# First squares on ScalarE, key-cache split spread over steps, samples' set-up later in each head: a hybrid decoder step on one core

## The chip, the cores and the metric

The kernel runs on one core of a Trainium2 chip. The metric is the device time of one execution, in microseconds (us); each comparison uses the median of several executions. Engines are named as the profile names them: PE is TensorE's matmul, PEld its weight load, DVE is VectorE, ACT is ScalarE, POOL is GpSimd, SP is SyncE, whose queue issues every DMA here.

## The reference

One layer of a decoder with three parallel branches is computed for a prompt of 1024 tokens and for 8 samples of 4 tokens, with the same weights, in float32. Cut to what matters:

```python
h = rmsnorm(x) * g;  p = h @ w_in      # ret q,k,v,g | sgu u,v | xattn q | 3 gates
A = silu(g) * groupnorm(retention(rope(q), rope(k), v))       # 4 heads, chunks of 128
B = gelu(u) * (tril(W_s) @ layernorm(gelu(v)) + b)            # per chunk of 128 positions
C = softmax(xq @ mem_k.T / sqrt(128)) @ mem_v                 # 4 heads, 256 memory rows
x = x + (sig(gA)*A@w_br_ret + sig(gB)*B@w_br_sg + sig(gC)*C@w_br_x) @ w_o
x = x + convffn(rmsnorm(x));   y = rmsnorm_final(x)
```

The mean square of x that the first norm needs is a sum over 1024 features, which lie on 8 tiles of 128 partitions. For the samples, retention starts from a given state of each head, and cross-attention reads a given cache of keys and values; both need masked copies of the samples' queries, one copy for each of the 8 samples.

## The kernel before

All 1056 tokens (1024 of the prompt, 32 of the samples) lie along the free dimension; features lie on partitions. Every float32 operand of a matmul is split into a rounded high part and a remainder, and a product takes three matmuls: high by high, high by low, low by high. The high part is a copy on ACT, the remainder a subtraction, for weights mostly on POOL (`w_prep`, lines 140 to 155: tiles `wh` and `wl`, three of each). The input is kept unnormalised in the split (`hh`, `hl` from the raw tiles `xr`, function `x_part`, lines 392 to 396); the reciprocal root `rst` of the mean square is multiplied in afterwards, when a product is taken out of the accumulation memory.

A product of 8 feature tiles is made by `fm`: eight steps of nine matmuls (three terms by three column chunks). After each step `hook()` is called. It runs deferred single operations (`later(n, ...)`, due after n hooks) and then, at the current `rate`, advances a queue of Python generators, `gens`, by one `yield` each. What lies between two yields of a generator is thus put between two steps of matmuls in PE's order and at that point of every other engine's order. [...] `drain()` runs the generators to their end.

The first two products, q and k of head 0, are interleaved by `fm2` over 16 steps, so that PE can follow the arrival of x. q's tile is complete at the 13th step and is then taken out by `rope_evac` (ACT copies `sw`, DVE multiplies by `cosT`, POOL multiplies `sw` by `sinT`, and DVE adds the two four hooks later). The tile pool for products, `mp`, has two buffers, so the third product, g of head 0, starts only once q's buffer has been read. The smaller pool `ap` has two buffers of one bank each.

In the ramp the sum of squares is made in two parts. Tiles 0 to 3 are squared and added on POOL, ahead of everything in `gens` (lines 408 to 411). Tiles 4 to 7 are squared on ACT and added on DVE inside the generator `xnorm` (lines 428 to 465), after `YA` empty yields; after `YB` further ones it forms `rst` by `rstd_all` (split the sum into `rsh` and `rsl`, three pairs of matmuls with a matrix of ones, three Newton operations on DVE), transposes it into `rtok`, takes g's tile out of the accumulation memory, and multiplies `q`, `k`, `cosT` and `sinT` by `rst`. During head 0 the rate is one yield per hook, and 32 hooks lie in q, k and the two g products. If g has not been taken out by then, lines 714 and 715 step `xnorm` until it has; then `drain()` runs the rest.

Each head's `retention` generator runs during the next head's products, at 25.5/32 of a yield per hook. Its operations are A (scores of two chunks; four DVE operations and one on ACT make the tile `rt`), B (one chunk's output and state), C (transposing two chunks back), and for the samples SA (set-up: masked scores, `kdm` on POOL, and in heads 0 to 2 the masked queries `qm3`, two DVE multiplications by a mask), SC (samples' products with the state; it reads `qm3`), SB and SD. B and SA are two of the operations that use the two `ap` buffers in turn. At each operation's start, deferred normalisations of earlier rows (DVE, after a POOL power) are issued first.

Before the cross-attention, `KS(0, 0)` and `KS(0, 1)` split the first key cache (ACT copies `kch`, POOL subtractions `kcl`) where they stand, after the product `sv`. `gens` then holds `sgu`, whose steps multiply on PE, add on DVE (`sgt`) and multiply on DVE (`su`), and `xattn(0)`, whose product YA is the first to read the keys. Three `xq` products and eight `gb` products, 88 hooks at 1.05 yields each, cover `sgu` and the four `xattn` generators.

Of the kernel before, what the change touches and what calls it, by code (L numbers as in the profile page):

```python
# [10 lines left out]
AF = mybir.ActivationFunctionType  # L11
ALU = mybir.AluOpType
# [66 lines left out]
def step_kernel(ctx: ExitStack, tc: tile.TileContext, xT, memT, wslab, cst, ident_d, rope, vec, sgc, sgm, sgs,  # L79
# [10 lines left out]
    def slot(name, dt=F32, shape=None):  # L90
        return sp.tile(shape or [P, T], dt, tag="S", name=name, bufs=NSLOT)
# [16 lines left out]
    def act(out, in_, func=AF.Identity, scale=1.0, bias=0.0, **kw):  # L108
        nc.scalar.activation(out=out, in_=in_, func=func, scale=scale, bias=bias, **kw)  # L109

    def vtt(out, a, b, op):
        nc.vector.tensor_tensor(out=out, in0=a, in1=b, op=op)  # L112

    def ptt(out, a, b, op):
        nc.gpsimd.tensor_tensor(out=out, in0=a, in1=b, op=op)  # L115
# [56 lines left out]
    gens = deque()  # L172
# [112 lines left out]
    def split(src, name, sub=ptt):  # L285
        shape = list(src.shape)
        hi = slot(name + "h", F32R, shape)
        lo = slot(name + "l", F32R, shape)
        nc.scalar.copy(out=hi, in_=src)
        sub(lo, src, f(hi), ALU.subtract)  # L290
        return hi, lo
# [60 lines left out]
    with tc.manual_schedule():  # L352
# [9 lines left out]
        xr = [slot("xr") for _ in range(8)]  # L362
# [43 lines left out]
            x_part(k, slice(0, T))  # L406

        for k in range(4):
            ptt(xr[k], xr[k], xr[k], ALU.mult)
            for a, b in {1: ((1, 0),), 3: ((3, 2), (3, 1))}.get(k, ()):  # L410
                ptt(xr[a], xr[a], xr[b], ALU.add)
        for i in range(2):
            hil[SLABS[i]] = first[i]
        wst.update(d=2, p=2, live=2)
# [8 lines left out]
        nc.vector.tensor_scalar(out=vecs[:, VBG:VBG + 32], in0=vecs[:, VBG:VBG + 32], scalar1=0.5, scalar2=None,  # L423
                                op0=ALU.mult)

        YA, YB = 5, 6

        def xnorm():
            for _ in range(YA):
# [64 lines left out]
        def retention(h, qt, kt, silu, V, st, s3, s0, s0s):  # L494
# [156 lines left out]
                    stt(ot[e][:, TP:T], a[:, e * 32:e * 32 + 32],  # L651
                        vecs[:, VGN + 2 * h + e:VGN + 2 * h + e + 1], silu[e][:, TP:T], ALU.mult, ALU.mult)

            for fn, *a in ((int,), (A, 0), (SA,), (A, 1), (B, 0), (B, 1), (SC, 0), (B, 2), (C, 0), (SC, 1), (A, 2), (B, 3),
                           (SB, 0), (B, 4), (C, 1), (A, 3), (B, 5), (SD,), (B, 6), (C, 2), (SB, 1), (B, 7),
                           (SB, 2), (SB, 3), (C, 3)):
                while defer:
                    defer.pop(0)()
                fn(*a)
                yield  # L660
# [37 lines left out]
        for h in range(H):  # L698
# [58 lines left out]
            tm((("v", h, 0), ("v", h, 1)), hops, v_evac, st[0:NSAMP, 256:512])  # L757
            drain()
            gens.append(retention(h, qt, kt, silu, V, st, s3, s0, s0s))


# [116 lines left out]
        def sgu():  # L878
            for _ in range(3):
                yield  # L880
            for half in range(2):
                for g in range(4):
                    a = ap()
                    for n in range(4):
                        mm(a[:, n * P:(n + 1) * P], vt(4 * half + n)[:, g * P:(g + 1) * P], sgW[:, g * P:(g + 1) * P])
                    t = slot("sgt")
                    vtt(t[:, 0:512].rearrange("p (a b) -> p a b", a=4), a.rearrange("p (a b) -> p a b", a=4),
                        sgC[:, g * P:(g + 1) * P].unsqueeze(1).to_broadcast([P, 4, P]), ALU.add)
                    s = su[g][:, half * 512:(half + 1) * 512]
                    vtt(s, s, t[:, 0:512], ALU.mult)  # L890
                    yield
                if half == 0:
                    vc_load(0)
            a = ap()
            for g in range(4):
                mm(a[:, g * 32:g * 32 + 32], sgS[0:32, 512 + g * P:512 + (g + 1) * P],
                   sgS[0:32, 256 + 32 * g:256 + 32 * g + 32])
            t = slot("sgt")
            vtt(t[:, 0:128], a[:, 0:128], sgC[:, 512:640], ALU.add)
            for g in range(4):  # L900
                ptt(su[g][:, TP:T], su[g][:, TP:T], t[:, g * 32:g * 32 + 32], ALU.mult)
                later(4, lambda g=g: dma(scr[8 + g], su[g]))
            yield
# [25 lines left out]
        def KS(h, i):  # L929
            if h < H:  # L930
                ksl.setdefault(h, {})[i] = split(kcl[h][i], "kc")
# [184 lines left out]
        later(4, lambda: dma(sgv, sgS[0:32, 512:1024]))  # L1116
        rate[0] = 1.05
        gens.append(sgu())
        KS(0, 0)
        KS(0, 1)  # L1120
        gens.append(xattn(0))
        for m in range(1, 4):
            xq_unit(m)
# [104 lines left out]
        def x_split(name, k, src, sub):  # L1228

            while len(X.setdefault(name, [])) <= k // 2:  # L1230
                X[name].append((slot("xh", F32R), slot("xl", F32R)))
            hi, lo = xop(name, k)
            nc.scalar.copy(out=hi, in_=src)
            if sub:
                sub(lo, src, f(hi), ALU.subtract)
# [27 lines left out]
        def h_scale(k, half):  # L1263
            stt(hs(k, half), hs(k, half), vecs[:, VNF + k:VNF + k + 1], rst[:, half * HW:(half + 1) * HW], ALU.mult, ALU.mult)
# [215 lines left out]
        A = lambda k: (h_scale(k, 1), x_split(B1(k), k % 4, h(k, 1), None))  # L1480
# [471 lines left out]
def build(shapes):  # L1952
    import concourse.bacc as _bacc

    nc = _bacc.Bacc("TRN2", target_bir_lowering=False, num_devices=1)
    args = [nc.dram_tensor(f"in_{n}", shapes[n], F32, kind="ExternalInput").ap() for n in _INS]
    args += [nc.dram_tensor(f"out_{n}", s, F32, kind="ExternalOutput").ap() for n, s in _OUTS]
    with tile.TileContext(nc) as tc:
        step_kernel(tc, *args)
    return nc  # L1960
# [22 lines left out]
```

## Time and profile before

| | us |
|---|---|
| median of 3 runs (1942.96 to 1952.96) | 1944.57 |
| the profiled execution's own time | 1949.1 |
| its span, first to last instruction | 1947.3 |
| PE busy | 1878.4 (96%) |
| DVE busy | 1078.1 (55%) |
| POOL busy | 927.7 (48%) |
| ACT busy | 615.9 (32%) |

A row of the timeline has the start and the length in microseconds, the engine, the line of the kernel, the operation, the tiles written and read, the shape and a count where equal instructions were merged (the length is then that of the whole series). In brackets stands how long the engine had been idle before it and whose work ended that. A row of a list of waits has the total, the number and the longest. A row by windows has the busy time of each engine in a stretch, then the granted TensorE clock as a share of full speed (PEclk).

### The profile page before, as it was taken

To read this page: it belongs to the slowest core of one execution; us is meant where nothing else is said; L and a number is where in the kernel's file an instruction comes from. 1 tells how busy PE (TensorE), PEld (TensorE's weight loads), DVE (VectorE), ACT (ScalarE), POOL (GpSimd) and SP (SyncE) were. 2 spreads that over 40 slices of the span, in tenths; PEclk is the share of its full clock that TensorE was granted. 3 is DMA by queue.
4 is the path that set the end of the run, shared out by engine and by line. 5 is a ranking of instruction groups with operands and counts; after the bars stand their busy time and mean duration, and the time that the engine had idled before them with its cause. 6 is when DMAs were issued, how large, how long until landed. Compare 5 with 4: busy or idle time off the path is not lost.

```text
span 1947.3 us, 31390 instructions
## 1 busy us (share of the span) xinstructions
PE 1878.4 (96%) x13201; PEld 1852.8 (95%) x13201; DVE 1078.1 (55%) x1506; ACT 615.9 (32%) x962; POOL 927.7 (48%) x576
## 2 busy tenths in 40 slices
PE   7999999999989999999999999899999999999997
PEld 6999999999989999999999999899999999999996
DVE  8463636443375541111112247999999999744446
ACT  5232232322234332111132233534434334321204
POOL 6242424232544334333154434477777777753404
PEclk9999999999999999999999999899999999999998
DMA  5112121324142313111221443022222222742202
GB/s 184 55 44 91 44 91 44 132 68 153 55 133 77 109 45 133 55 44 54 89 84 48 164 153 99 33 66 89 77 66 89 77 84 95 264 142 89 75 1 90
DMA packets 51741, 174.51 MB, mean 90 GB/s; under 512 B 5712, under 2 KB 8944, under 8 KB 51600
## 3 DMA queue, kind: packets, MB, share of 16 engines
q1 hardware_dynamic: 51600, 172.50, 26.3%
q8 instruction: 104, 1.70, 0.4%
q14 instruction: 37, 0.30, 0.1%
HBM read 137.04 MB, written 35.43 MB: 89 GB/s over the span
## 4 chain that ended last, share of the span: by engine, by line
PE 80%; DVE 11%; ACT 3%; issue 3%; DMA 1%; POOL 1%; SPq 0%; DVEq 0%; ACTq 0%; POOLq 0%
PE mp L106 55%; PE bp L106 20%; PE ap L106 4%; DVE xl L112 1%; DVE c L118 1%; DVE x2c L118 1%; DVE hl L118 1%; DVE s L112 1%; DMA xr<-in_xT 1%; DMA scr<-ox 0%; ACT sw L476 0%; DVE rt L118 0%; DVE st L526 0%; SPq L103 0%; PE ap L576 0%
## 5 line engine op out<-in xcount | busy, mean ns | idle before, releaser
L115 POOL TENSOR_TENSOR wl<-wr,wh 128x1024 fp32r<-128x1024 f32 x114 | 296.7, 2605 | 463.6 <-ACT wh L150 391.2
L106 PE MATMUL mp<-hh,wh 128*128 128x384 f32 (+1 forms) x1152 | 264.2, 337 | 9.7 <-DVE q L112 4.9
L106 PE MATMUL mp<-hl,wh 128*128 128x384 f32 (+1 forms) x1152 | 254.1, 328 | 4.8 <-DVE hl L118 4.8
L106 PE MATMUL mp<-hh,wl 128*128 128x384 f32 (+1 forms) x1152 | 251.8, 326 | 0.0
L106 PE MATMUL bp<-xh,wh 128*128 128x264 f32 (+2 forms) x1040 | 211.4, 284 | 1.0 <-DVE x2c L118 0.9
L106 PE MATMUL bp<-xl,wh 128*128 128x264 f32 (+2 forms) x1040 | 211.1, 284 | 0.0
L106 PE MATMUL bp<-xh,wl 128*128 128x264 f32 (+2 forms) x1040 | 211.0, 284 | 0.0
L106 PEld LDWEIGHTS mp<-hh,wh 128*128 128x128 f32 x1152 | 192.9, 192 | 12.9 <-ACT hh L109 5.3
L106 PEld LDWEIGHTS mp<-hl,wh 128*128 128x128 f32 x1152 | 193.5, 190 | 7.2 <-DVE hl L118 7.2
L106 PEld LDWEIGHTS mp<-hh,wl 128*128 128x128 f32 x1152 | 193.8, 190 | 0.0
L112 DVE TENSOR_TENSOR x<-x,mp 128x288 f32<-128x288 f32 (+3 forms) x167 | 105.7, 675 | 121.3 <-PE mp L106 121.3
L106 PEld LDWEIGHTS bp<-xh,wh 128*128 128x128 f32 x1040 | 162.4, 188 | 1.4 <-issue 1.4
L106 PEld LDWEIGHTS bp<-xl,wh 128*128 128x128 f32 x1040 | 162.4, 188 | 0.0
L106 PEld LDWEIGHTS bp<-xh,wl 128*128 128x128 f32 x1040 | 162.3, 188 | 0.0
L115 POOL TENSOR_TENSOR wl<-fs,wh 128x1024 fp32r<-128x1024 f32 x41 | 119.0, 2902 | 55.7 <-ACT wh L1295 55.7
L150 ACT CAST wh<-wr 128x1024 fp32r<-128x1024 f32 x100 | 103.9, 1041 | 78.7 <-PE mp L106 50.0
L106 PE MATMUL mp<-ach,whs 128*128 128x384 f32 (+3 forms) x524 | 124.3, 326 | 3.9 <-DVE x L112 3.1
L118 DVE SCALAR_TENSOR_TENSOR c<-z,hist,c 128x1024 f32<-128x1024 f32 x88 | 124.6, 1416 | 4.2 <-ACT c L109 2.5
L112 DVE TENSOR_TENSOR th<-mp,rst 128x768 f32<-128x768 f32 (+1 forms) x48 | 31.6, 701 | 170.9 <-PE mp L106 150.3
L106 PE MATMUL mp<-acl,whs 128*128 128x384 f32 (+3 forms) x524 | 124.1, 327 | 0.0
L106 PE MATMUL mp<-ach,wls 128*128 128x384 f32 (+3 forms) x524 | 124.0, 326 | 0.0
L118 DVE SCALAR_TENSOR_TENSOR th<-th,mp 128x768 f32<-128x768 f32 (+1 forms) x48 | 31.7, 701 | 145.4 <-PE mp L106 145.4
(356 smaller groups left out, 4107.9 us busy)
## 6 DMA issues: line engine op xcount, KB each, us to landing
wr<-in_wslab SPq DMA_DIRECT2D x162, 512.0 KB, 3.6
sca<-c SPq DMA_DIRECT2D x22, 528.0 KB, 3.0
opr<-sca SPq DMA_DIRECT2D x22, 528.0 KB, 4.5
opr<-scr SPq DMA_DIRECT2D x16, 528.0 KB, 5.4
scr<-ort SPq DMA_DIRECT2D x8, 528.0 KB, 7.6
x2c<-in_xT SPq DMA_DIRECT2D x8, 528.0 KB, 7.7
scx<-x2c SPq DMA_DIRECT2D x16, 264.0 KB, 3.5
x<-scx SPq DMA_DIRECT2D x8, 528.0 KB, 6.9
```

Of the source, the lines that this page charges most:

```text
L106: nc.tensor.matmul(out=out, lhsT=l, rhs=r, start=start, stop=stop)
L112: nc.vector.tensor_tensor(out=out, in0=a, in1=b, op=op)
L115: nc.gpsimd.tensor_tensor(out=out, in0=a, in1=b, op=op)
L118: nc.vector.scalar_tensor_tensor(out=out, in0=a, scalar=s, in1=b, op0=op0, op1=op1)
L150: nc.scalar.copy(out=hi, in_=raw)
```

## The change

Three places change. In the ramp, tiles 0 to 3 are squared on ACT instead of POOL and added on DVE instead of POOL; `xnorm` starts its own squares after 14 yields instead of 5, which is the second yield after q's tile is complete, and waits 3 yields instead of 6 before `rstd_all`. In each head the samples' set-up SA comes after both score operations and the first B instead of between the two A. In the cross-attention the split of the first key cache becomes a generator with two yields after each half, placed between `sgu` and `xattn(0)`.

```diff
         for k in range(4):
-            ptt(xr[k], xr[k], xr[k], ALU.mult)
+            act(xr[k], xr[k], AF.Square)
             for a, b in {1: ((1, 0),), 3: ((3, 2), (3, 1))}.get(k, ()):
-                ptt(xr[a], xr[a], xr[b], ALU.add)
+                vtt(xr[a], xr[a], xr[b], ALU.add)
...
-        YA, YB = 5, 6
+        YA, YB = 14, 3
...
-            for fn, *a in ((int,), (A, 0), (SA,), (A, 1), (B, 0), (B, 1), (SC, 0), (B, 2), (C, 0), (SC, 1), (A, 2), (B, 3),
+            for fn, *a in ((int,), (A, 0), (A, 1), (B, 0), (SA,), (B, 1), (SC, 0), (B, 2), (C, 0), (SC, 1), (A, 2), (B, 3),
...
         gens.append(sgu())
-        KS(0, 0)
-        KS(0, 1)
+
+        def first_keys():
+            for i in range(2):
+                KS(0, i)
+                yield
+                yield
+
+        gens.append(first_keys())
         gens.append(xattn(0))
```

## The prediction

> **What bounds the kernel.** I read the page's chain first, then the list of what PE waited for, then the timeline around each wait that the change touches, engine by engine.
>
> ```profile
> PE 80%; DVE 11%; ACT 3%; issue 3%; DMA 1%; POOL 1%; SPq 0%; DVEq 0%; ACTq 0%; POOLq 0%
> ...
> PE ap L106 <- DVE sgt L112: 7.6, 1, 7.6
> ...
> PE ap L106 <- DVE rt L118: 5.4, 3, 2.6
> PE mp L106 <- DVE q L112: 4.9, 1, 4.9
> ...
> PE mp L106 <- DVE hl L118: 4.8, 7, 1.7
> ```
>
> PE sets the time, so an edit is worth what it takes from PE's waits. The four rows are the waits that the change aims at: the masked products of `sgu`, the heads' `rt`, q's eviction and the splits of x. All four are waits for DVE.
>
> **The ramp, what goes away.** The rows are the timeline's, then one stretch by windows.
>
> ```profile
> 10.78 1.32 DVE L118 SCALAR_TENSOR_TENSOR hl<-xr,vecs,hh 128x1056 fp32r<-128x1056 f32 x1 [0.46 <-ACT hh L109]
> 12.18 18.90 POOL L115 TENSOR_TENSOR xr<-xr 128x1056 f32<-128x1056 f32 x6 [2.81 <-DVE hl L118]
> 13.23 18.96 DVE L118 SCALAR_TENSOR_TENSOR hl<-xr,vecs,hh 128x1056 fp32r<-128x1056 f32 x6
> 18.61 1.18 ACT L109 ACTIVATE hh<-xr,vecs 128x1056 fp32r<-128x1056 f32 x1
> ...
> 13.24 0.65 PE L106 MATMUL mp<-hh,wh 128*128 128x384 f32 x3
> 14.70 0.64 PE L106 MATMUL mp<-hh,wh 128*128 128x384 f32 x3
> 37.23 0.65 PE L106 MATMUL mp<-hh,wl 128*128 128x384 f32 x3
> 42.76 1.22 PE L106 MATMUL mp<-hh,wh 128*128 128x384 f32 x3 [4.89 <-DVE q L112]
> ...
> 42.00:48.00 6.00, 5.24 (x18) 5.27 (x19) 5.99 (x6) 5.00 (x7) 4.83 (x3) 0.50 0.28 87
> ```
>
> One split `hl` takes 1.32 with POOL idle. The six that run beside POOL's six squares and additions take 18.96, 3.16 each, and POOL's 3.15 each: the two engines take turns. Without POOL's six, the splits follow ACT's `hh`, whose last ends at 18.61 + 1.18 = 19.8, so the last split ends near 21.2 instead of 32.2. PE's steps are 14.70 - 13.24 = 1.46 apart. Twelve remain from 14.70, so q and k would end at 32.2; they end half a microsecond after 37.23, at 37.7. The earlier splits bring **5.5**. The new `hl` times (14.6, 15.9, 17.3, 18.6, 19.9, 21.2) are all ahead of the steps that read them, the next of which start at 15.2, 17.6 and 19.1.
>
> PE then waits until 42.76 for q's eviction, which stands behind DVE's additions: **5.0**. After the wait the clock is granted at 0.50 (42.00 to 48.00), with PE busy for 5.24: half of that, **2.6**, is lost too. Together 13.1.
>
> **The ramp, what comes.** The moved work is four squares and seven additions in all, and its order decides.
>
> ```profile
> 22.43 1.09 ACT L109 ACTIVATE xr<-xr 128x1056 f32<-128x1056 f32 x1 [2.64 <-DVE hl L118]
> 33.22 1.04 ACT L150 CAST wh<-wr 128x1024 fp32r<-128x1024 f32 x1
> 34.29 2.19 ACT L476 COPY sw<-mp 64x768 f32<-64x768 f32 x4
> ...
> 34.34 2.55 POOL L115 TENSOR_TENSOR wl<-wr,wh 128x1024 fp32r<-128x1024 f32 x1 [3.26 <-ACT wh L150]
> 36.85 3.42 POOL L115 TENSOR_TENSOR sw<-sw,sinT 128x1056 f32<-128x1056 f32 x1
> ...
> 41.31 1.31 DVE L112 TENSOR_TENSOR q<-mp,cosT 128x768 f32<-128x768 f32 x2
> ...
> 156.11 0.95 PE L106 MATMUL ap<-V,rt 128*128 128x256 f32 x6 [1.99 <-DVE ort L118]
> ...
> 157.40:160.90 3.50, 3.50 (x14) 3.50 (x13) 1.83 (x5) 0.37 (x1) 0.74 (x2) 0.51 0.51 206
> ```
>
> The first four squares, 1.09 each, run on ACT from 19.8 to 24.2, and the three additions at some 1.25 on DVE until about 29, the last held up by POOL's next weight split. q's tile is complete at 27.8; ACT's four copies (2.19) end at 30.1, DVE's eviction (1.31) at 30.5, both before 32.2. So g starts without a wait, with 1.7 to spare; if that cover went, each microsecond later would be one lost.
>
> From there I place the instructions in the new order, with 2.45 for a POOL operation and 1.25 for a DVE one, taking turns. ACT: a cast until 31.1, two squares until 33.3, k's copies until 35.5, a cast until 36.6, two squares until 38.7. POOL: weight split until 35.0, k's `sw` until 38.7, weight split until 42.3. DVE, each behind POOL's current one: first addition 36.2, k's eviction 37.6, q's sum 39.9, addition 43.6, two more 46.1, k's sum 47.3, `rsl` 48.5. In PE's order the matmuls of ones come after the ninth step from 32.2, at 45.3. They **wait 3.2**. This wait is new, since `xnorm` has been moved back by 6 yields. Its bounds: 0 if DVE need not wait for POOL (five additions of 1.25 and `rsl` end before 45), 7 if all seven operations take a turn of 3.3.
>
> The other end of `xnorm` moves as well: it needs 34 yields to g's eviction, and there are 32 hooks. The last transposes and that eviction come after all matmuls of the second g, and the next product needs g's buffer: copies of `rtok`, then 1.3 for the eviction as for q, **1.8** (bounds 1.3 and 3).
>
> [...] The ramp: 13.1 - 3.2 - 1.8 - 1.3 = **6.8**, between 2 and 11.5.
>
> [...]
>
> **The heads.** In heads 0 to 2, A, B and SA each move into the next one's place in PE's order.
>
> ```profile
> 101.51 4.93 POOL L115 TENSOR_TENSOR wl<-wr,wh 128x1024 fp32r<-128x1024 f32 x2 [13.88 <-ACT wh L150]
> 106.69 1.90 POOL L115 TENSOR_TENSOR kdm<-s,cB 96x1024 fp32r<-96x1024 f32 x1 [0.26 <-DVE s L112]
> ...
> 104.11 0.18 DVE L112 TENSOR_TENSOR st<-ap,cB 96x32 f32<-96x32 f32 x1
> 105.07 1.54 DVE L112 TENSOR_TENSOR s<-st,s 32x160 fp32r<-32x160 f32 x1 [0.79 <-ACT s L592]
> 106.75 2.46 DVE L112 TENSOR_TENSOR s<-s,cB 128x256 fp32r<-128x256 f32 x2
> 109.13 0.47 DVE L118 SCALAR_TENSOR_TENSOR rt<-ap,cB 128x256 fp32r<-128x256 f32 x1
> 110.43 0.42 DVE L112 TENSOR_TENSOR rt<-rt,cB 128x256 fp32r<-128x256 f32 x1
> 110.76 0.42 DVE L568 COPY Sst<-ap 128x256 f32<-128x256 f32 x1
> 113.21 0.42 DVE L526 TENSOR_SCALAR cB<-cB,mv,grs 128x256 f32<-128x256 f32 x1 [0.94 <-POOL grs L115]
> ...
> 106.98 0.87 PE L106 MATMUL ap<-V,rt 128*128 128x256 f32 x6
> 113.33 0.28 PE L106 MATMUL ap<-s0h,s 128*64 128x256 f32 x1
> ```
>
> SA holds DVE from 104.11 to 109.2, and the second A's `rt` follows it; the second B waits for its buffer. Moving SA removes these waits: 5.4 in three heads, and clock of about 1.1 expected for the one of 2.6. What is late next is SC, which reads the masked queries. In head 0 the second `rt` ends at 106.8 (its last operation behind POOL's splits, 101.51 + 4.93 = 106.4). B's row work with its normalisation, which is issued ahead of SA and waits for POOL's power, takes 113.63 - 110.76 = 2.9: 109.7. SA's chain took 5.1, of which 1.2 was the operation at 105.07 behind the weight split: 3.9, to 113.6, with `kdm` before the masked queries as now. SC stands at 113.33 less the removed wait of 1.4, 111.9: it waits 1.7. By the same steps head 2 waits about 2.2, head 1 about 0.5 (first B, `rt` not ready) and 1.6: 6.0 in all, with clock 2.4. The edit is worth 5.4 + 1.1 - 6.0 - 2.4 = **-1.9**, bounds +6.5 (no wait at SC) and -6 (1.4 more per head). Head 3 makes no split queries and no PE wait of it is listed: nothing.
>
> **The first keys.**
>
> ```profile
> 537.54 1.28 POOL L115 TENSOR_TENSOR sgS<-sgS,sgW 32x512 f32<-32x512 f32 x1 [0.71 <-DVE sgS L874]
> 538.79 4.66 POOL L115 TENSOR_TENSOR kcl<-kc,kch 128x1024 fp32r<-128x1024 f32 x2
> 543.42 4.62 POOL L115 TENSOR_TENSOR wl<-wr,wh 128x1024 fp32r<-128x1024 f32 x2
> ...
> 538.03 10.57 DVE L112 TENSOR_TENSOR su<-su,sgt 128x512 f32<-128x512 f32 x1
> ...
> 549.25 2.08 PE L106 MATMUL ap<-sgW,vg 128*128 128x128 f32 x8 [7.58 <-DVE sgt L112]
> ...
> 549.20:553.40 4.20, 4.15 (x16) 4.15 (x17) 3.37 (x5) 0.23 (x1) 0.00 (x0) 0.50 0.80 242
> ```
>
> A DVE multiplication that needs 0.7 stands for 10.57, from inside POOL's `sgS` until POOL's whole series ends at 548.0: here there is no taking of turns. PE waits 7.58 and then runs at 0.50 for 4.2, losing 2.1: 9.7. Without `kcl` the two weight splits follow `sgS` at 538.8 and end at 543.4, so the multiplication ends at 544.0 and the next eviction at 544.7; PE, done at 541.7, waits 3.1 plus clock 1.3. Gain 9.7 - 4.4 = **5.3**; bounds 9.7 (turns) and 0. The two `kcl`, 4.66, come behind `sgu`'s last step, two yields apart, when DVE has only q's split and mask for `xattn`; I take 0 there, since the first comes four steps ahead of these, and up to 2.5 if a POOL operation holds them up. The tail fits: `xattn` moves back four yields, 92 of 92.4, and no DMA goes past another queue's work in time to matter (the caches of the second head are loaded from within `xattn`, tens of microseconds ahead of use).
>
> **Sum.** 6.8 - 1.9 + 5.3 = 10.2, 0.5% of the span of 1947.3. The profiled execution took 1949.1, the median of the runs is 1944.6, 4.5 lower, as profiled executions lie here; I take the same 10.2 from the median: **1934.5**.
>
> **Rivals.**
> 1. *DVE always gets its turn, and the new waits stay away.* The ramp's rows (3.16 and 3.15) speak for it, the 10.57 against. The keys then give 9.7, and the ones wait 1 instead of 3.2 with no clock: 10.2 + 4.4 + 3.5 = 18.1, 1926.5. Chance 0.2. [...]
> 2. [...] Chance 0.08.
> 3. *The starving only moves.* The multiplication still waits out a series (a next weight split arrives before POOL is idle), or `kcl` holds up q's split for `xattn` instead: the keys give 0 and the sum is 4.9, 1939.7. Chance 0.17.
> 4. *The squares are not the brake:* the splits `hl` stay near 3 beside full DMA traffic. The row at 10.78, 1.32 under the same traffic, speaks against it. Then 5.5 is missing: 1940. Chance 0.05.
> 5. *Slower: the samples' set-up starves in its new place.* Its four DVE operations with two SBUF inputs each meet one more POOL operation of 2.5 behind `kdm`: three more than counted, 7.4, on a wait of 2, with clock 11 per head, 33 in three heads against 6.5 now: 1944.6 - 12.1 + 26.8 = 1959.3. It decides from 6.2 per head, clock included. For it speaks the 10.57, against it that POOL has only short operations queued there. Chance 0.05.
>
> The forecast has the remaining 0.45; its own range is 1930 to 1940. A difference of 0.5%, 9.7, is about what can be told from no change here. Rivals 1 and 2 and half of the forecast's cases lie below 1934.9: faster 0.5; the rest of it and rivals 3 and 4, 0.44; slower 0.06. The range 1925 to 1943 holds all but rival 5 and the ends of the others.
>
> **What would show it.** Right: six `hl` of 1.3 and no PE wait for `hl` after 13 us; no wait for `q`; a new wait of the ones matmuls (`rsl`) of about 3; waits for `rt` gone and waits for `s` of about 2 at SC; the wait for `sgt` near 3. Wrong: a `su` that starves as long as before, a wait for `rst` at the transposes, a wait at `xattn(0)`'s first product, or no half clock after waits of 2 to 3.

## The result, and the profile after

The median of 7 runs is 1935.95 us (1934.9 to 1939.26), against 1945.64 for the kernel before on the same chip. The ratio is 0.9942, with a 95% interval of 0.993 to 0.9953: 9.7 us faster by the medians and 11.3 by the ratio, where 10.2 was forecast. The profiled execution after took 1936.22, its span 1934.4, which is 12.9 less than the span before. That is more than the medians give, because the profiled execution before was a long one: 1949.1, 3.5 above the median of its kernel, where the one after lies 0.3 above.

From the page after, the chain that ended last:

```profile
PE 81%; DVE 11%; ACT 4%; issue 3%; POOL 1%; DMA 1%; DVEq 0%; SPq 0%; ACTq 0%; POOLq 0%
```

PE still sets the time. From the list of what PE waited for, after:

```profile
PE ap L106 <- DVE s L112: 4.3, 3, 1.6
...
PE ap L106 <- DVE xql L112: 3.7, 2, 2.1
...
PE ap L106 <- DVE sgt L112: 3.0, 1, 3.0
...
PE mp L106 <- DVE silu L112: 1.5, 1, 1.5
PE ap L106 <- DVE pt L112: 1.5, 3, 0.9
PE ap L106 <- ACT rsh L333: 1.4, 1, 1.4
...
PE ap L106 <- DVE rsl L112: 0.9, 1, 0.9
```

The waits for `q`, `hl` and `rt` are gone and the one for `sgt` fell from 7.6 to 3.0. The rows for `s`, `silu`, `rsh` and `rsl` are the new waits that were forecast. The row for `xql` was not forecast.

To see where the time went, I cut the span at three places that every kernel here has: the first matmul of head 0's value product (`mp<-wh,hh`, the end of the ramp), the eviction of the samples' last half of `sgu`'s v (`sgC<-mp`, the end of the heads), and the first matmul of the product behind the cross-attention (`mp<-oph`, the end of the keys). These are rows of the timeline of the kernel before, with the first matmul ahead of them:

```profile
4.84 0.69 PE L106 MATMUL mp<-hh,wh 128*128 128x384 f32 x1 [4.84 <-ACT hh L109]
...
70.58 0.28 PE L106 MATMUL mp<-wh,hh 128*128 128x256 f32 x1
...
493.83 0.41 DVE L112 TENSOR_TENSOR sgC<-mp,sgC 32x256 f32<-32x256 f32 x1 [24.04 <-ACT sgC L278]
...
752.50 0.34 PE L106 MATMUL mp<-oph,wh 128*128 128x384 f32 x1
```

and of the kernel after:

```profile
5.83 0.69 PE L106 MATMUL mp<-hh,wh 128*128 128x384 f32 x1 [5.83 <-ACT hh L109]
...
63.71 0.39 PE L106 MATMUL mp<-wh,hh 128*128 128x256 f32 x1 [1.53 <-DVE silu L112]
...
482.71 0.41 DVE L112 TENSOR_TENSOR sgC<-mp,sgC 32x256 f32<-32x256 f32 x1 [24.15 <-ACT sgC L278]
...
738.50 0.34 PE L106 MATMUL mp<-oph,wh 128*128 128x384 f32 x1
```

| stage | before | after | difference | forecast |
|---|---|---|---|---|
| start, to the first matmul | 4.84 | 5.83 | +1.0 | 0 |
| ramp | 65.74 | 57.88 | -7.9 | -6.8 |
| heads | 423.25 | 419.00 | -4.3 | +1.9 |
| keys | 258.67 | 255.79 | -2.9 | -5.3 |
| rest, to the end of the span | 1194.8 | 1195.9 | +1.1 | 0 |

A stage's length moves by some 2 us between profiled executions of kernels in which it is the same; over all 14 profiled here the ramp takes 64.2 to 65.8 in its old form and 56.4 to 58.6 in its new one (the squares alone left aside), the heads 421.3 to 423.8 and 418.9 to 420.5. So the two signs are no accident of one trace. The other two rows are within the noise: the first matmul starts anywhere from 4.8 to 5.8, and the rest, which no kernel here edits, takes 1191.7 to 1198.7.

The total came out close, but of its three terms the heads were wrong in sign and the keys in size, and the two errors nearly cancel.

**The ramp after.** The timeline of DVE, and then that of PE, at the places named in the prediction:

```profile
13.56 7.93 DVE L118 SCALAR_TENSOR_TENSOR hl<-xr,vecs,hh 128x1056 fp32r<-128x1056 f32 x6
...
30.53 1.32 DVE L112 TENSOR_TENSOR q<-mp,cosT 128x768 f32<-128x768 f32 x2 [1.75 <-ACT sw L476]
...
47.10 1.26 DVE L112 TENSOR_TENSOR rsl<-xr,rsh 128x1056 fp32r<-128x1056 f32 x1
```

```profile
47.12 0.44 PE L106 MATMUL ap<-rsh,ones 128*128 128x384 f32 x1 [1.42 <-ACT rsh L333]
48.42 0.44 PE L106 MATMUL ap<-rsl,ones 128*128 128x384 f32 x1 [0.85 <-DVE rsl L112]
```

Six splits `hl` take 7.93, or 1.32 each, and the last ends at 21.5 (forecast 21.2). q's eviction ends at 31.85, ahead of PE. `rsl` ends at 48.36 (forecast 48.5). The matmuls of ones wait 1.42 + 0.85 = 2.3 in place of 3.2, since PE arrives at 45.7 rather than 45.3 and has 0.44 of matmuls on `rsh` to do before it needs `rsl`, and g's eviction makes the next product wait 1.53 in place of 1.8.

**The keys after.** POOL's timeline and then DVE's, at the series that held up `su`:

```profile
526.44 1.27 POOL L115 TENSOR_TENSOR sgS<-sgS,sgW 32x512 f32<-32x512 f32 x1 [0.71 <-DVE sgS L874]
527.68 4.69 POOL L115 TENSOR_TENSOR wl<-wr,wh 128x1024 fp32r<-128x1024 f32 x2
```

```profile
526.93 5.99 DVE L112 TENSOR_TENSOR su<-su,sgt 128x512 f32<-128x512 f32 x1
```

As forecast, `su` waits out `sgS` and both weight splits: it ends at 526.93 + 5.99 = 532.92, 0.55 behind the end of the second split at 532.37, and one such multiplication takes 0.69 when nothing holds it up. The wait for `sgt` is 2.95, forecast 3.1.

### The profile page after: what moved, and what is told of

The parts are those of the page before. It is cut to its first block, busy times and chain, and to the rows that moved or that the text cites. A ratio compares the mean times of both kernels' runs of the same rounds, so it can differ in the third digit from the quotient of the medians.

```text
span 1934.4 us, 31394 instructions
## 1 busy us (share of the span) xinstructions
PE 1873.5 (97%) x13201; PEld 1849.0 (96%) x13201; DVE 1064.7 (55%) x1509; ACT 620.0 (32%) x966; POOL 904.3 (47%) x569
## 4 chain that ended last, share of the span: by engine, by line
PE 81%; DVE 11%; ACT 4%; issue 3%; POOL 1%; DMA 1%; DVEq 0%; SPq 0%; ACTq 0%; POOLq 0%
PE mp L106 56%; PE bp L106 20%; PE ap L106 4%; DVE xl L112 1%; DVE c L118 1%; DVE x2c L118 1%; ACT sw L476 1%; ACT wh L150 0%; DMA sca<-c 0%; DVE st L526 0%; DVE ssf L112 0%; DVE rt L118 0%; PE ap L576 0%; DVE th L112 0%; DVE rt L112 0%
```

## The experiments

Each kernel is timed in turn with the kernel before on the same chip, and the ratio goes by those runs. Five isolate parts of the change, three look at the starving, and four vary the changed kernel.

**The ramp alone**, the first two hunks of the change on the kernel before.

> The kernel before with the ramp's part alone (squares of tiles 0 to 3 on ACT, additions on DVE, 14 and 3 empty yields). Theory (the forecast's terms): 6.8 us faster, with new waits of the ones matmuls (2 to 3) and of about 1.5 for g's eviction. Rival (the parts only work together, because the starting point of the later stages shifts against each other): under 4 or over 10.

Measured: 1940.42 against 1947.23, ratio 0.9957 (0.9944 to 0.9971): 6.8 less by the medians, 8.4 by the ratio. In its trace the ramp is 56.38 long, 9.4 less than before; the waits are those of the changed kernel, 1.4 + 0.9 at the ones and 1.5 at g's eviction, but no half clock follows them, and the ramp is 1.5 shorter than in the changed kernel. The forecast of the ramp stands.

**The squares alone**, with `xnorm` where it was:

```diff
-            ptt(xr[k], xr[k], xr[k], ALU.mult)
+            act(xr[k], xr[k], AF.Square)
...
-                ptt(xr[a], xr[a], xr[b], ALU.add)
+                vtt(xr[a], xr[a], xr[b], ALU.add)
```

> The kernel before with the squares on ACT and the additions on DVE, but the empty yields left at 5 and 6. Theory: the splits hl speed up as in the full change (5.5); q's eviction then stands behind seven additions and comes at 35 to 36, so PE waits 3 to 4 for it with a loss of clock, and nothing waits at the ones or at the end of g: 7 to 8.5 us faster, as much as with the moved yields or more. Rival (moving the later squares behind the eviction is what pays): 3 us faster or less, with a wait for q near 5 as before.

Measured: 1942.86, ratio 0.9979 (0.9971 to 0.9988), 4 us less than before. I had expected more. What PE waited for in its first 100 us, and the two ends of the ramp in PE's timeline:

```profile
PE mp L106 <- DVE q L112: 4.7, 1, 4.7
PE mp L106 <- DVE hl L118: 0.3, 1, 0.3
```

```profile
4.78 0.69 PE L106 MATMUL mp<-hh,wh 128*128 128x384 f32 x1 [4.78 <-ACT hh L109]
...
64.74 0.28 PE L106 MATMUL mp<-wh,hh 128*128 128x256 f32 x1
```

The ramp takes 59.96, 5.8 less than before. The part ahead of the wait for q takes 27.6 in place of 33.0, 5.4 less: the term of 5.5 for the splits, confirmed by itself. But q's eviction still stands behind DVE's additions, and PE waits 4.7 for it. So the order behind q's eviction is a part of its own, worth the 2.1 between 59.96 and 57.88 in the traces (3.6 against the 56.38 of the ramp alone) and 2.4 (medians) to 4.3 (ratios) in the timed runs. The forecast's terms for it were 5.0 + 2.6 gained and 3.2 + 1.8 + 1.3 given back, 1.3 net.

**The heads alone:**

```diff
-            for fn, *a in ((int,), (A, 0), (SA,), (A, 1), (B, 0), (B, 1), (SC, 0), ...
+            for fn, *a in ((int,), (A, 0), (A, 1), (B, 0), (SA,), (B, 1), (SC, 0), ...
```

> The kernel before with SA moved in the heads and nothing else. Theory (forecast): the waits for rt (5.4) become waits for the masked queries at SC (about 4.5 to 6), so -1.9 to +1 us. Rival (the new order frees the path, the waits at SC being covered): 4 to 6.5 us faster.

Measured: 1944.45, ratio 0.9987 (0.9978 to 0.9996): 2.5 us faster, where 1.9 slower was forecast. From the list of waits of PE, from PE's timeline and from DVE's:

```profile
PE ap L106 <- DVE s L112: 4.3, 3, 1.6
...
PE ap L576 <- DVE bst L522: 1.8, 2, 1.6
```

```profile
69.84 0.28 PE L106 MATMUL mp<-wh,hh 128*128 128x256 f32 x1
```

```profile
489.87 0.41 DVE L112 TENSOR_TENSOR sgC<-mp,sgC 32x256 f32<-32x256 f32 x1 [24.05 <-ACT sgC L278]
```

The stage takes 420.03, 3.2 less than before. The samples' products now wait 4.3 in three heads, and the waits for `bst` are 0.6 more in all than before: 4.9 for the 5.4 of `rt`, so half a microsecond of waiting is gained. The rest is clock. The next rows are windows from 100 to 400 us (busy time of PE, PEld, DVE, ACT and POOL, then the granted clock), of the kernel before, of this one, and of the changed kernel:

```profile
100.00:400.00 300.00, 288.03 (x2012) 282.86 (x2011) 158.47 (x304) 91.39 (x162) 108.45 (x91) 0.98 0.23 75
```

```profile
100.00:400.00 300.00, 288.31 (x2027) 282.76 (x2027) 157.56 (x310) 91.47 (x162) 108.27 (x93) 0.99 0.24 77
```

```profile
100.00:400.00 300.00, 288.31 (x2025) 281.50 (x2025) 154.29 (x305) 89.40 (x159) 105.88 (x93) 1.00 0.24 76
```

Before, the clock falls to half three times here, for some 3.5 us each (0.51 from 157.40 to 160.90, 0.53 from 205.00 to 208.60, 0.50 from 345.20 to 348.60); in this kernel once (0.50 from 155.90 to 159.30), and in the changed kernel never (1.00 over the 300 us). I estimate the cost of each as half of some 3.4 us at 0.50, 1.7. The first of the three stands behind the wait of 1.99 at 156.11, the other two behind these rows of PE's timeline before:

```profile
205.69 1.62 PE L106 MATMUL ap<-V,rt 128*128 128x256 f32 x6 [2.64 <-DVE rt L118]
...
343.73 0.94 PE L106 MATMUL ap<-V,rt 128*128 128x256 f32 x6 [1.99 <-DVE ort L118]
```

Only the one at 205.69 is a wait that the edit removes, and the new waits, of at most 1.6, are not followed by a half clock (in the changed kernel the clock is 1.00 from 104 to 115, 200 to 206 and 288 to 300 us, around its three waits for `s` of 1.57, 1.15 and 1.56). The two waits of 2.0 for `ort` stand in all 14 profiled kernels. In the eight with the old order a half clock followed 15 of these 16 waits, in the six with the new order 3 of 12: before, 0.51 and 0.50 behind the two, in the heads alone 0.50 behind the first, in the changed kernel 1.00 throughout. So the new order spares clock behind waits that it does not touch; why is not shown. Nor does the wait for `rt` of 2.6 always cost clock: of the eight kernels that have it, a half clock followed in three, among them the kernel before (0.53).

**The keys alone**, the last hunk of the change.

> The kernel before with the first keys' split moved and nothing else. Theory (forecast): the wait for sgt falls from 7.6 to about 3 and 5.3 us are gained. Rival (read from the trace after: the four yields by which the cross-attention moves back give part of it away in waits for xql): 2 to 3.5 us faster.

Measured: 1946.69, ratio 0.9997 (0.9988 to 1.0006): nothing that can be measured. PE's waits from 500 to 800 us, and the two ends of the stage:

```profile
PE ap L106 <- DVE xql L112: 3.7, 2, 2.1
PE ap L106 <- DVE sgt L112: 3.0, 1, 3.0
PE ap L106 <- DVE pt L112: 1.5, 3, 0.9
```

```profile
494.61 0.41 DVE L112 TENSOR_TENSOR sgC<-mp,sgC 32x256 f32<-32x256 f32 x1 [24.04 <-ACT sgC L278]
...
749.01 0.34 PE L106 MATMUL mp<-oph,wh 128*128 128x384 f32 x1
```

The wait for `sgt` falls by 4.6, much as forecast (from 7.6 to 3.1), and the stage is 254.40 long, 4.3 less than before. But 3.7 of waits for `xql` stand in the second and third cross-attention, where before had 0.5 in all, and `pt` has 1.5 where it had 0.4. On the other side, the waits for `ox` and `y`, 2.9 together before, are gone, so that the waits behind `sgu` are 1.6 more in all. Two theories were left: the four added yields shift the cross-attention against POOL's weight and key splits, and that costs; or the time is lost by chance of the clock.

**The keys without the shift**, on the kernel before: the two halves are split inside `sgu`, and no yield is added.

```diff
                     vtt(s, s, t[:, 0:512], ALU.mult)
+                    if half and g % 2:
+                        KS(0, g // 2)
                     yield
...
-        KS(0, 0)
-        KS(0, 1)
```

> The kernel before, with the two halves of the first key cache split at the sixth and the last full step of sgu, and no yield added, so that the cross-attention keeps its place among the steps of PE. Theory (the four added yields moved the cross-attention and so cost what the keys won): the wait for sgt falls from 7.6 to about 3 to 4, no xql wait over 0.6, time 4 to 5 us below the kernel before, ratio 0.9975. Rival (the place of the cross-attention does not matter, the gain is given back by clock phase or later buffers): as the keys alone with four yields, ratio 0.999 to 1.0 in spite of the smaller sgt wait.

Measured: 1941.73 against 1947.76, ratio 0.997 (0.9959 to 0.9981): 6 us less. The same two views:

```profile
PE ap L106 <- DVE sgt L112: 3.0, 1, 3.0
...
PE ap L106 <- DVE xql L112: 0.5, 1, 0.5
PE ap L106 <- DVE pt L112: 0.4, 1, 0.4
```

```profile
492.98 0.41 DVE L112 TENSOR_TENSOR sgC<-mp,sgC 32x256 f32<-32x256 f32 x1 [24.05 <-ACT sgC L278]
...
745.01 0.34 PE L106 MATMUL mp<-oph,wh 128*128 128x384 f32 x1
```

The wait for `sgt` is the same 3.0, the `xql` waits are back at 0.5, and the stage is 252.03: 6.6 less than before and 2.4 less than with the yields. The intervals of the two ratios do not meet. So the forecast's 5.3 was there to be had, and the kernel with the four yields lacks most of it. Of the 0.27% between the ratios, 5 us, the stage shows 2.4, about the 2.2 by which the waits in it differ; where the rest lies, these profiles do not show. The two kernels also differ in where the key splits stand. The waits make the shift the likely cause, but it is not the only difference.

**The queries first.** In the changed kernel, each later head's query split is issued ahead of that head's key splits:

```diff
-  (YC, 0), (XC, 2), (KS, h + 1, 0), (XB, 3), (YC, 1), (KS, h + 1, 1), (XC, 3), (QS, h + 1), (YD,)
+  (YC, 0), (XC, 2), (QS, h + 1), (KS, h + 1, 0), (XB, 3), (YC, 1), (KS, h + 1, 1), (XC, 3), (YD,)
```

> The changed kernel, with each later head's query split issued ahead of the split of that head's two key caches instead of behind both. Theory (the keys' missing gain is spent in the cross-attention, whose later phase puts the query split behind a key subtraction on POOL): the two waits of PE for xql, 2.1 and 1.7, go, the rest stays; 3 to 4 us less than the changed kernel, ratio to the kernel before near 0.9923. Rival (these waits only take the place of others, which come back when they go, or clock phase gave the time back): the xql waits go, waits for pt, ox or y of about the same sum come, ratio near 0.994 as for the changed kernel.

Measured: 1934.41, ratio 0.9932 (0.992 to 0.9945), 0.1% better than the changed kernel's ratio and not told apart from it. The `xql` waits are gone, and as the rival said, others came, though not of the same sum. Of PE's waits from 500 to 800 us:

```profile
PE ap L106 <- DVE pt L112: 3.5, 3, 2.3
```

Now `pt` is late where `xql` was: 3.5 are left of the 5.2 for both. In the trace the keys' stage, from 484.25 to 735.92, is 251.67 long, 4.1 less than in the changed kernel, and 1.7 of that is a half clock behind the wait for `sgt` that did not come here (1.00 from 533 to 545 us). So the order within the cross-attention is a part of the cause at most; for the rest that leaves its place among the steps, which the keys inside `sgu` kept.

**Does the 32-partition operation start the starving?** One theory had `su` starve simply because POOL's series follows without a gap. The other had the multiplication of the 32 samples' rows, with which the series begins, keep the engines from taking turns. In three kernels that row operation is done on DVE; two of them put a dummy operation in its place on POOL, on 32 and on 128 partitions.

```diff
-            ptt(v, v, sgW[0:M, 512:1024], ALU.mult)
+            (ptt if t < 8 else vtt)(v, v, sgW[0:M, 512:1024], ALU.mult)
```

> The kernel before, with the one multiplication on 32 partitions (sgS by sgW, 1.28 on POOL at 537.5) moved to DVE; POOL's series behind it (two kcl, two weight splits, 9.3 in all) stays. Theory 1 (DVE starves behind any back-to-back series of POOL): su still stands for 8 to 10 and PE waits 6 to 8 for sgt. Theory 2 (only a POOL operation on a part of the partitions keeps the two engines from taking turns): su takes at most 3.2, each POOL operation is delayed by a DVE one, and the wait for sgt is under 2.

> As the run with the 32-partition multiplication on DVE, plus one added POOL multiplication on 32 partitions and 512 columns in the old place, whose result nobody reads. Theory 1: starving as in that run, whichever it is. Theory 2: the starving is back, su 8 to 10.

> The same with the added POOL multiplication on 128 partitions instead of 32. Theory 1: no difference between this and the 32-partition one. Theory 2: su takes at most 3.2 and PE waits under 2 for sgt.

Measured in one execution each: 1947.89, 1952.08 and 1947.08, against 1948.5 for before; PE's wait for `sgt` is 8.4, 9.4 and 9.4. From the first of the three, POOL's timeline and then DVE's:

```profile
535.36 4.68 POOL L115 TENSOR_TENSOR kcl<-kc,kch 128x1024 fp32r<-128x1024 f32 x2
540.01 4.62 POOL L115 TENSOR_TENSOR wl<-wr,wh 128x1024 fp32r<-128x1024 f32 x2
```

```profile
535.42 9.50 DVE L874 TENSOR_SCALAR sgS<-sgS,lmv,lrs 32x512 f32<-32x512 f32 x1 [0.65 <-POOL lrs L115]
```

Without the row operation on POOL, the DVE operation that comes next stands through the four others for 9.50; it is not `su` now, as the expectation had it, but the normalisation of the samples' rows, which has one tile as input. In the two with a dummy it stands for 10.47 and 10.46. The second theory falls. The first holds for this series, but it is not a general rule: in the ramp before, splits of 3.16 and POOL operations of 3.15 did take turns.

**The series made shorter.** In the changed kernel, the remainders of two of the `xq` weight slabs, the two `wl` of 527.68, are subtracted on DVE:

```diff
-LO_DVE = [...] + [("sv", 0, 0), ("sv", 0, 1)]
+LO_DVE = [...] + [("sv", 0, 0), ("sv", 0, 1), ("xq", 2), ("xq", 3)]
```

> The changed kernel, with the remainders of the weight slabs xq 2 and xq 3 subtracted on DVE instead of POOL. These are the two POOL operations of 2.4 behind which the first su of sgu still stands for 6.0. Theory (su stands until POOL has nothing more queued): su takes 0.7 to 1.9, the sgt wait falls from 3.0 to under 1, its half clock of 3.4 us goes: 3.0 + 1.7 less, at most 1 for the two subtractions on DVE ahead of the first eviction; 3 to 4.5 us below the changed kernel, ratio near 0.9922. Rival (the su starves from another cause than POOL's queue): su stays over 4, ratio 0.994.

Measured: 1934.22, ratio 0.9933 (0.9919 to 0.9947). In the trace both steps came: the wait for `sgt` is 0.9 and no half clock follows it (1.00 from 500 to 600 us, where the changed kernel has 0.98), and the keys' stage is 252.25, 3.5 less than in the changed kernel. The half clock alone is 1.7 of these 3.5. In the timed runs the gain over the changed kernel is 0.1%, less than the intervals.

```profile
PE ap L106 <- DVE sgt L112: 0.9, 1, 0.9
```

**Both of these edits:**

> The changed kernel with both edits: query split ahead of the key split, and the remainders of xq 2 and xq 3 on DVE. If both theories hold the gains add: 6 to 8 us below the changed kernel, ratio to the kernel before near 0.990, time near 1927. If only one holds, 3 to 4 us and a ratio near 0.992; if none, 0.994.

Measured: 1932.4, ratio 0.9924 (0.9912 to 0.9937), about half of what was expected if both theories held: 0.18% better than the changed kernel's ratio. One reason can be read from the traces: the gains of both edits, 4.1 and 3.5, hold the same half clock of 1.7 behind the wait for `sgt`, which can be saved only once. With both edits the stage takes 251.17.

**The best parts together:** the changed ramp and heads, the keys inside `sgu`, the two remainders on DVE.

> The changed kernel with the first key cache split at the sixth and the last full step of sgu (no yield added), and the remainders of the weight slabs xq 2 and xq 3 on DVE. Theory (the parts act on different waits, so their gains add): ramp and heads as in the changed kernel (-0.43 and -0.13 per cent), the keys as measured inside sgu (-0.30), the remainders -0.09 to -0.18: ratio 0.990 to 0.9905, time near 1927; PE waits for sgt under 1, for xql and pt together under 1.5. Rival (with the earlier steps of sgu the key subtractions on POOL meet other work again): ratio 0.992 as with the four yields, with a wait over 1.5 for sgt, xql or pt between 500 and 800 us.

Measured: 1931.97 against 1948.01, ratio 0.9914 (0.99 to 0.9927), the best kernel here: 16 us below before and 4 (medians) to 5 (ratios) below the changed kernel. The waits came as the theory had them, 0.9 for `sgt` and 0.9 for `xql` and `pt` together, but the ratio lies between the theory's 0.990 to 0.9905 and the rival's 0.992. Its keys' stage is the shortest of all:

```profile
482.46 0.41 DVE L112 TENSOR_TENSOR sgC<-mp,sgC 32x256 f32<-32x256 f32 x1 [24.14 <-ACT sgC L278]
...
732.22 0.34 PE L106 MATMUL mp<-oph,wh 128*128 128x384 f32 x1
```

249.76, 6.0 less than in the changed kernel. Yet its whole span is only 3.5 less. The windows from 1160 to 1290 us, far behind any edit, show where some of it went: of before, of the changed kernel, and of this one.

```profile
1160.00:1290.00 130.00, 117.96 (x935) 116.79 (x935) 114.28 (x136) 60.92 (x100) 65.77 (x40) 0.96 0.21 70
```

```profile
1160.00:1290.00 130.00, 118.07 (x927) 116.99 (x926) 114.57 (x139) 60.23 (x100) 66.29 (x43) 0.95 0.20 69
```

```profile
1160.00:1290.00 130.00, 117.49 (x908) 116.91 (x909) 110.94 (x138) 61.33 (x103) 67.09 (x45) 0.93 0.19 62
```

The granted clock is 0.96, 0.95 and 0.93. I estimate the loss from these as 130 times 0.04, 0.05 and 0.07: 5.2, 6.5 and 9.1. Nothing in these instructions was edited; they only run earlier. Windows that begin equally far behind the end of the keys give the same picture: 1.00, 0.98 and 0.95 over 70 us from 400 us behind it. But running earlier is not enough: the kernel with the queries first ends its keys 2.6 us ahead of the changed kernel and has 0.97 from 1200 to 1300 us, where the changed kernel has 0.95. That is one execution of each kernel, so I call it what these profiles show and not a law.

## Why the prediction was right, and where it was not

**The ramp: right.** Forecast -6.8; -7.9 in the trace, -6.8 to -8.4 alone. The 5.5 for the splits is confirmed by the squares alone, with 5.4. Two terms were too large: the wait of the ones matmuls (3.2, measured 2.3) and g's eviction (1.8, measured 1.53). No run shows the clock term of 1.3: the runs had a half clock of some 1.7 or none. It came in four of the six profiled kernels with the new ramp (the first 100 us are at 0.98 in the changed kernel, with the queries first and with the best parts together), not in the ramp alone nor with the remainders on DVE (1.00). From 49.2 us on, the window of the changed kernel has it at half:

```profile
49.20:52.60 3.40, 3.40 (x14) 3.40 (x13) 0.72 (x2) 1.28 (x3) 3.40 (x15) 0.51 0.26 37
```

That is some 1.7 by the same estimate, behind two waits that make 2.3 together.

**The heads: wrong in sign.** The mechanism was right: `rt` waits vanish, SC waits come. The steps that failed are two sizes. "6.0 in all" measured 4.3, and 0.6 for `bst`; and "with clock 2.4" measured nothing: every new wait is at most 1.6, and the changed kernel has a clock of 1.00 from 100 to 400 us. In "worth 5.4 + 1.1" the clock of the one wait of 2.6 was 1.7 in the trace before, with 0.53 behind it. So no run shows these two clock terms, 1.1 and 2.4. With 5.4 + 1.7 - 4.9 the edit is worth 2.2 in place of -1.9, and alone it was 2.5 faster. The traces show more, 3.2 alone and 4.3 in the full change, since half clocks behind the `ort` waits are gone there too (one and two of 1.7), which the prediction did not have and these runs do not explain.

**The keys: right where they were worked out, wrong where they were taken at nothing.** The wait for `sgt` came at 3.0 for 3.1. What failed is "I take 0 there" and "`xattn` moves back four yields, 92 of 92.4": I checked that the moved generator still fits and that its first head is not held up, and did not look for what its later heads would meet. There `xql` and `pt` wait 4.3 more, `ox` and `y` 2.9 less, and in all PE waits 5.6 behind `sgu` where it waited 4.0 before. Those 1.6 lie within the bound of 2.5, but the keys alone, with 0.03% in the timed runs, miss nearly all of the 5.3, and what is lost beyond this stage is not located. No run shows the clock term of 1.3 here either: the changed kernel has a half clock of some 1.7, and the window behind its `sgt` wait is at 0.54; the keys alone, the keys inside `sgu` and the queries first have none behind the same wait of 3.0, each with 1.00 from 500 to 600 us.

```profile
533.60:537.30 3.70, 3.70 (x15) 3.70 (x16) 3.24 (x5) 0.01 (x1) 0.00 (x0) 0.54 0.84 306
```

**The rivals.** The first falls: DVE got no turn at 526.93, where its 0.69 became 5.99. The second, that the new waits leave the clock at full, falls by the two windows just shown: 0.51 behind waits of 2.3 together, 0.54 behind one of 2.95. But length does not decide alone: with the queries first the same wait, 3.0 in the list, ended at 535.12 and was followed by a clock of 1.00.

```profile
533.00:545.00 12.00, 9.88 (x72) 9.88 (x73) 11.56 (x15) 2.02 (x2) 3.30 (x2) 1.00 0.62 222
```

The third, that the starving only moves, was half right: `su` was relieved, but q's split for the cross-attention was held up instead, in later heads than named, and for the keys alone the gain of 0 that it gave is what was measured. The fourth falls with splits of 1.32, the fifth with SC waits of 1.6.

**The total.** The shares of the three parts alone, -0.43, -0.13 and -0.03 per cent, add to -0.59, and the full change has -0.58 (the three intervals are up to 0.14 wide on each side). So the sum of 10.2 was right by cancelling, which is luck: the heads gave some 4 to 6 more than forecast, the keys 2 to 5 less. (Two slips of arithmetic in the prediction change nothing: 1944.6 - 10.2 is 1934.4, and the fifth rival's 33 - 6.5 is 26.5.)

## What to carry to other kernels

When work is taken out of one place by adding steps to a list, cost the shift of everything behind it, not just whether it still fits; a variant that moves the work without moving the rest is the test. Short waits on the bounding engine are to be priced with the clock that may follow: in the heads, single waits of up to 1.6 were followed by no half clock (1.00 in the changed kernel), while those of 2.0 to 2.6 were in some kernels and not in others (0.50 to 0.53 before, 1.00 behind those of 2.0 in the changed kernel), so that their price is an expectation and one trace does not settle it. And when parts are forecast separately, test them separately, since a right total can hide two wrong terms.

## What the runs showed of the hardware

At the start of `sgu`, DVE's operations did not take turns with POOL's series: 5.99 over three POOL operations after, 10.57 over five before, 9.50 over four with the row operation on DVE, this last one with a single tile as input. One of POOL's operations was longer, too: in the best parts together, which have the two remainders on DVE, `sgS` at 526.20 takes 3.25, where it takes 1.27 in the changed kernel. So DVE's operation stood through three to five POOL operations in a row here, and in the ramp before through one at a time (3.16 beside POOL's 3.15). What decides between the two was not found.
